# The exponents of an mLSTM: one row spread over the partitions, and columns in ScalarE's bias

## The chip, the cores and the metric

The kernel runs on one core of a Trainium2 chip. The metric is the time of one execution on the device in microseconds; the time of before is the median of three runs.

## The reference

One layer of a streaming encoder over a prompt of 2048 tokens and a batch of 8 sequences with 16 new tokens each (128 sample tokens). Model width 1024. An input projection feeds two groups of heads, the mLSTM matrix memory (4 heads of 128) and sliding-window attention (8 query heads of 64); then an output projection, LayerNorm, a convolutional feed-forward of width 2816, LayerNorm. What the change touches is the matrix memory. For one chunk, with gates `li`, `lf` per token and head and the carried state `C`, `n`, `m`:

```python
b = jnp.cumsum(lf, axis=-1)
inter = b + m[..., None]
dmat = jnp.where(causal, b[..., :, None] - b[..., None, :] + li[..., None, :], -jnp.inf)
mt = jnp.maximum(inter, jnp.max(dmat, axis=-1))
w_inter = jnp.exp(inter - mt)
s = jnp.einsum('bhld,bhsd->bhls', qc, kc) * jnp.exp(dmat - mt[..., None])
num = w_inter[..., None] * jnp.einsum('bhld,bhde->bhle', qc, C) + jnp.einsum('bhls,bhse->bhle', s, vc)
den = w_inter * jnp.einsum('bhld,bhd->bhl', qc, n) + jnp.sum(s, axis=-1)
h = num / jnp.maximum(jnp.abs(den), jnp.exp(-mt))[..., None]
```

With a = li - b and M = mt - b, three exponents are needed: a[s] - M[l] under the causal mask (128 keys by 128 queries by 4 heads), m - M[l] (the same for every partition), and -(b + M)[l]. The state goes on with the last column of the first two.

## The kernel before

The 2048 prompt tokens are 16 tiles of 128 (the kernel takes chunks of 128 tokens), the sample tokens are tile 16. `BLOCKS` groups the tiles into five input blocks, `[16, 0, 1]` first. For each block `i_block` makes the input projection: dense products of 384, 512 or 256 columns on TensorE, three passes each (`mm3`, lines 207 to 209) with operands split into a high and a low fp32r part. Then `o_block` makes the output projection per block, and the feed-forward follows (`f_ups`, `f_downs`).

The order on TensorE is written by hand. `Chains.weave` steps through the dense products and, by an estimated time, takes steps of three generators in between: `t_sample` (tile 16, first), `m_chain` (matrix memory of the prompt tiles) and `a_chain` (attention of the prompt tiles). Their `yield` gives how much of TensorE's time a step is taken for and how long its successor shall wait. VectorE, ScalarE, GpSimd and the DMA issues on SyncE are ordered by a scheduler; each engine then works through its list in order.

PSUM: the dense products rotate over three banks (`dps`); everything in the chains takes one of five banks with one tag (`bank`, tag `tb`). A tile of PSUM may be written when the bank's former content has been read.

One prompt tile of the matrix memory:

- `m_rows` transposes the gates to rows of 4 partitions x 128 (`pgr`), and VectorE scans `b`, `a`, `M` (lines 627 to 629). `hilo_rows` (564, 565) writes a in two fp32r parts into `ae` and the carried m into `me`; `hilo_rhs` (571, 572) splits M into `r_Mh` and `r_Ml`, and GpSimd multiplies each by a diagonal pattern into `re` (574, 575), which is 100 x 512. `emt_row` (579) makes the row `y` = -(b + M).
- `m_tile` loads q, k, v (`m_load`), makes the scores (`pscore`, 672) and the transposed keys (`pkt`, 683), then the exponents as one product each of 100 rows by 512 columns: `m_inter` (664, bank named `pe2`, written `pe` in the trace) for m - M, and `m_weights` (654, `pe`) for a - M. ScalarE takes the exponential of the first into `wi` (666); VectorE takes the minimum of the second and the mask into `dt` (656), ScalarE its exponential (657). `emt_cols` (585, bank `pemt`) turns `y` into columns. VectorE makes `sd` = scores x `dt` (677) and `kw` = keys x last column of `dt` (738), GpSimd `qk` = q x `wi` (736).
- After further dense work: the numerators (`pnum`, 745 and 746), the state update (`pcu`, 753, and `C`, 756), `m_norm`, and `m_out` (`pht`, 721, copied by ScalarE into `mixm`, 723).

An attention tile takes the banks `pq`, `pk` (768, 770), four `psc` for its scores, reduced on VectorE with the mask (`amx`, 815), `ppt` for transposed weights (835) and `ppo` (842, 843). Weights for the dense products are split by ScalarE (`whi`, 202) and VectorE (`wlo`, 203); `xh`, `xl` (348, 349) are the split inputs. `d_sums` (`tx`, `ty`) prepares weights of the down projection on VectorE along the way.

Of the kernel before, what the change touches and what calls it, by code (L numbers as in the profile page):

```python
# [23 lines left out]
MH = 4  # L24
# [26 lines left out]
def _consts():  # L51
    c = {}
    c["ident"] = np.eye(P, dtype=np.float32)
    l = np.arange(P)
    c["mcau"] = np.where(l[:, None] <= l[None, :], 0.0, NEG).astype(np.float32)
    c["mblk"] = np.where((l[:, None] <= l[None, :]) & (l[:, None] // DS == l[None, :] // DS), 0.0, NEG).astype(np.float32)
    ch = l[:, None] // 64
    kc = l[None, :] // 64
    own = np.where(kc <= ch, 0.0, NEG)
    prev = np.where(kc >= ch, 0.0, NEG)  # L60
    c["mswa"] = np.stack([np.concatenate([prev, own], 1), np.concatenate([own, prev], 1)], 1).astype(np.float32)
    half = 32
# [5 lines left out]
    d4 = np.zeros((MH, MH, P), np.float32)  # L68
    for h in range(MH):
        d4[h, h] = 1.0  # L70
    c["delta"] = -d4
    oz = np.zeros((100, P), np.float32)
    oz[0:4] = 1.0
    oz[96:100] = 1.0
    c["onesz"] = oz
    dz = np.zeros((100, MH, P), np.float32)
    dz[32:36] = d4
    dz[64:68] = d4
    c["deltaz"] = dz
# [110 lines left out]
class Prog:  # L190
# [295 lines left out]
    def t_setup(self):  # L486
        nc, a, tp = self.nc, self.a, self.tp

        def ld(n):
            t = self.one("k_" + n, list(a[n].shape))  # L490
            nc.sync.dma_start(t, a[n])
            return t
        nc.sync.dma_start(self.ident, a["ident"])
        self.gb = ld("gb")
        self.mcau = ld("mcau")
        self.mblk = ld("mblk")
        self.mswa = ld("mswa")
        self.delta = ld("delta")
# [4 lines left out]
        oz = self.work("hn", [100, P])  # L503
        nc.sync.dma_start(oz, a["onesz"])
        dz = self.work("kw", [100, MH, P])
        nc.sync.dma_start(dz, a["deltaz"])

        self.ae, self.me, self.re = [], [], []
        for i in range(2):
            for l, n, src, sh in ((self.ae, "ae", oz, [100, P]), (self.me, "me", oz, [100, P]), (self.re, "re", dz, [100, MH, P])):  # L510
                t = self.one(f"{n}{i}", sh, F32R)
                nc.vector.tensor_copy(t, src)
                l.append(t)
# [44 lines left out]
        self.nc.tensor.transpose(ps[:, 1], g[:, i, 4:8], self.ident)  # L558
        return ps[:, 0], ps[:, 1]

    def hilo_rows(self, dst, src):

        nc = self.nc
        nc.vector.tensor_copy(dst[32:36], src)
        nc.vector.tensor_sub(dst[64:68], src, dst[32:36].bitcast(F32))

    def hilo_rhs(self, re, M):

        nc = self.nc
        h, l = self.row("Mh", F32R), self.row("Ml")  # L570
        nc.vector.tensor_copy(h, M)
        nc.vector.tensor_sub(l, M, h.bitcast(F32))
        bc = lambda r: r.rearrange("p (o m) -> p o m", o=1).to_broadcast([MH, MH, P])
        nc.gpsimd.tensor_tensor(re[0:4], bc(h.bitcast(F32)), self.delta, op=ALU.mult)
        nc.gpsimd.tensor_tensor(re[96:100], bc(l), self.delta, op=ALU.mult)

    def emt_row(self, b, M):
        y = self.row("y")
        self.nc.vector.scalar_tensor_tensor(y, b, -1.0, M, op0=ALU.mult, op1=ALU.subtract)
        return y  # L580

    def emt_cols(self, y):

        ps = self.bank([P, MH], "pemt")
        self.nc.tensor.transpose(ps, y, self.ident[:MH, :MH])
# [37 lines left out]
    def m_rows(self, t, b, ti):  # L623
        V = self.nc.vector
        lf, li = self.gate_rows(self.logs_of(b), ti)
        bc, a_, M = self.row("b"), self.row("a"), self.row("M")
# [8 lines left out]
        self.mc = self.work("mc", [MH, 1], bufs=3)  # L635
        V.tensor_add(self.mc, bc[:, P - 1:P], M[:, P - 1:P])
        return ae, me, re, y

    def m_load(self, t, b, ti):
        nc = self.nc  # L640
# [6 lines left out]
        nc.sync.dma_start(og, self.zog[t].rearrange("p (h e) -> p h e", h=MH))  # L647
        return qk, v1, og

    def m_weights(self, ae, re, mask):  # L650

        nc = self.nc
        pe = self.bank([P, MH, P], "pe")
        nc.tensor.matmul(pe.rearrange("p h l -> p (h l)"), ae, re.rearrange("p h l -> p (h l)"), start=True, stop=True)
        dt = self.work("dt", [P, MH, P])
        nc.vector.tensor_tensor(dt, pe, mask.rearrange("p (o m) -> p o m", o=1).to_broadcast([P, MH, P]), op=ALU.min)
        nc.scalar.activation(dt, dt, AF.Exp)
        return dt

    def m_inter(self, me, re):  # L660

        nc = self.nc
        pe = self.bank([P, MH, P], "pe2")
        nc.tensor.matmul(pe.rearrange("p h l -> p (h l)"), me, re.rearrange("p h l -> p (h l)"), start=True, stop=True)
        wi = self.work("wi", [P, MH, P])
        nc.scalar.activation(wi, pe, AF.Exp)
        return wi

    def m_scores(self, qk):
# [53 lines left out]
        nc.scalar.copy(mix, ps)  # L723
        self.mix_out(t, 0, mix)

    def m_tile(self, t, b, ti, ae, me, re, y):
# [124 lines left out]
    def t_sample(self):  # L851
        nc, a = self.nc, self.a
        V = nc.vector
        t = NPT
# [6 lines left out]
        bc, a_, M, ar = [self.row(n) for n in ("b", "a", "M", "x")]  # L861
# [12 lines left out]
        self.hilo_rhs(self.re[0], x)  # L874
        self.hilo_rows(self.ae[1], a_)
        self.hilo_rhs(self.re[1], M)
        y = self.emt_row(bc, M)
# [40 lines left out]
        hn = self.m_norm(num, emt, og)  # L918
# [612 lines left out]
```

## Time and profile before

| | us |
|---|---|
| median of three runs | 2494.75 (2488.86 to 2495.19) |
| profiled execution | 2496.35 |
| its span | 2494.6 |
| TensorE busy | 2395.8 (96%) |
| VectorE busy | 1865.9 (75%) |
| ScalarE busy | 1205.2 (48%) |
| GpSimd busy | 467.2 (19%) |

The first 860 us hold the input projection, the output projection of four blocks and the three chains; the rest is the feed-forward. In the profile's rows PE is TensorE, PEld its weight loads, DVE VectorE, ACT ScalarE, POOL GpSimd, SP SyncE. A row of a timeline gives start, length, engine, line, operation and the tile written with the tiles read; in brackets stands idle time of the engine before it and what ended it. Lengths of matmuls include their latency; what one takes from the next is seen from start to start. The lines of waits give the waiting group, the releaser, the total, the count and the longest.

### The profile page before, as it was taken

The numbers are of one execution on the slowest core, as the hardware profiler recorded it, in microseconds if no ns is written. First come the engines' busy times: TensorE is split into PE (matmuls) and PEld (weight loads), VectorE is DVE, ScalarE is ACT, GpSimd is POOL, SyncE is SP. The second block draws the span as 40 slices with busy tenths as digits, with TensorE's granted clock in tenths as the row PEclk, the third lists the DMA queues.
The fourth block names the chain that finished last, engine by engine and source line by source line (L and its number), as shares of the span: only waits on it lengthen the run. The fifth ranks groups of instructions, "written<-read, shape, count | busy, mean of one in ns | idle before, by whom it ended". The sixth has DMA issues, their size and how long they took to land.

```text
span 2494.6 us, 36890 instructions
## 1 busy us (share of the span) xinstructions
PE 2395.8 (96%) x12922; PEld 2131.1 (85%) x12922; DVE 1865.9 (75%) x3244; ACT 1205.2 (48%) x2170; POOL 467.2 (19%) x486
## 2 busy tenths in 40 slices
PE   8999999999989899989999999999999999999998
PEld 8777778878887777789999999999999978778776
DVE  5656777487588887888788876678766677796897
ACT  4323445344355543555555545555544544444553
POOL 1211332132143434310000000002000010220300
PEclk9999999999998999999999999999999999999999
DMA  8886744544556567667777789886998876656653
GB/s 268 306 275 221 249 128 136 174 125 136 176 163 204 174 205 261 212 227 271 288 279 264 264 301 315 314 304 223 326 300 262 267 267 205 232 188 203 219 185 108
DMA packets 277117, 575.28 MB, mean 231 GB/s; under 512 B 45300, under 2 KB 122204, under 8 KB 276932
## 3 DMA queue, kind: packets, MB, share of 16 engines
q1 hardware_dynamic: 275204, 566.64, 67.3%
q0 software_dynamic: 1728, 6.29, 0.7%
q8 instruction: 102, 1.67, 0.3%
q14 instruction: 83, 0.68, 0.1%
HBM read 419.06 MB, written 153.78 MB: 230 GB/s over the span
## 4 chain that ended last, share of the span: by engine, by line
PE 54%; DVE 10%; issue 4%; DMA 3%; ACT 3%; POOL 2%; SPq 0%; DVEq 0%; ACTq 0%; POOLq 0%
PE dps L1240 16%; PE fup L1240 15%; PE fht L1437 5%; PE dps L1437 5%; PE fup L1437 5%; PE dps L207 2%; PE dps L209 2%; PE dps L208 2%; DVE wlo L203 2%; DMA zf<-cc 1%; ACT cc L1286 1%; DVE cc L1288 1%; DVE hl L203 1%; PE fht L1112 0%; POOL ymix L1028 0%
## 5 line engine op out<-in xcount | busy, mean ns | idle before, releaser
L1240 PE MATMUL fup<-hh,uw 128*128 128x384 f32 (+1 forms) x1848 | 483.6, 330 | 10.8 <-ACT u L1265 3.5
L1240 PE MATMUL dps<-hh,uw 128*128 128x384 f32 (+1 forms) x1848 | 481.7, 329 | 7.4 <-ACT u L1265 5.1
L203 DVE TENSOR_TENSOR wlo<-wraw,whi 128x1024 fp32r<-128x1024 f32 (+3 forms) x289 | 349.0, 1215 | 143.8 <-ACT whi L202 137.2
L202 ACT CAST whi<-wraw 128x1024 fp32r<-128x1024 f32 (+3 forms) x289 | 281.8, 981 | 310.4 <-PE dps L1437 94.0
L1240 PEld LDWEIGHTS fup<-hh,uw 128*128 128x128 f32 x1848 | 331.8, 189 | 13.9 <-ACT u L1265 4.7
L1240 PEld LDWEIGHTS dps<-hh,uw 128*128 128x128 f32 x1848 | 330.6, 188 | 9.6 <-ACT u L1265 6.6
L1288 DVE SCALAR_TENSOR_TENSOR cc<-u,cw,cc 128x768 f32<-128x768 f32 (+1 forms) x264 | 252.6, 977 | 110.6 <-ACT cc L1286 108.2
L207 PE MATMUL dps<-whi,xh 128*128 128x512 f32 (+1 forms) x816 | 317.3, 389 | 0.0
L209 PE MATMUL dps<-whi,xl 128*128 128x512 f32 (+1 forms) x816 | 310.5, 380 | 2.3 <-DVE xl L349 2.3
L208 PE MATMUL dps<-wlo,xh 128*128 128x512 f32 (+1 forms) x816 | 310.5, 380 | 2.1 <-DVE wlo L203 2.0
L1240 PE MATMUL fup<-hl,uw 128*128 128x384 f32 (+1 forms) x924 | 303.7, 329 | 1.4 <-DVE hl L203 1.4
L1240 PE MATMUL dps<-hl,uw 128*128 128x384 f32 (+1 forms) x924 | 302.7, 328 | 0.0
L1286 ACT ACTIVATE cc<-u,cw 128x768 f32<-128x768 f32 (+1 forms) x132 | 129.6, 997 | 117.7 <-DVE u L1279 58.1
L209 PEld LDWEIGHTS dps<-whi,xl 128*128 128x128 f32 x816 | 155.1, 190 | 34.1 <-DVE xl L349 2.7
L208 PEld LDWEIGHTS dps<-wlo,xh 128*128 128x128 f32 x816 | 155.7, 191 | 31.4 <-DVE wlo L203 2.9
L207 PEld LDWEIGHTS dps<-whi,xh 128*128 128x128 f32 x816 | 155.8, 191 | 30.1 <-ACT xh L348 0.4
L1240 PEld LDWEIGHTS fup<-hl,uw 128*128 128x128 f32 x924 | 174.4, 189 | 1.6 <-DVE hl L203 1.6
L1240 PEld LDWEIGHTS dps<-hl,uw 128*128 128x128 f32 x924 | 173.9, 188 | 0.0
L1437 PE MATMUL fup<-whi,fu 128*128 128x512 f32 x484 | 159.6, 402 | 6.4 <-DVE yacc L1466 4.4
L1437 PE MATMUL dps<-whi,fu 128*128 128x512 f32 x440 | 149.0, 395 | 0.0
L1280 POOL COPY u<-prev 128x4 f32<-128x4 f32 x66 | 45.3, 687 | 465.2 <-DVE cc L1288 449.9
L1437 PE MATMUL fht<-whi,fu 128*128 128x512 f32 x396 | 132.1, 396 | 0.2 <-DVE yacc L1466 0.2
(289 smaller groups left out, 4598.7 us busy)
## 6 DMA issues: line engine op xcount, KB each, us to landing
uw<-zw SPq DMA_DIRECT2D x176, 512.0 KB, 4.7
zw<-uw SPq DMA_DIRECT2D x88, 512.0 KB, 2.9
wv<-wup SPq DMA_DIRECT2D x66, 512.0 KB, 5.6
wraw<-wtm SPq DMA_DIRECT2D x60, 512.0 KB, 4.8
wraw<-zt SPq DMA_DIRECT2D x60, 512.0 KB, 4.2
wraw<-wdn SPq DMA_DIRECT2D x45, 512.0 KB, 4.0
wraw<-wqk SPq DMA_DIRECT2D x40, 512.0 KB, 5.0
wraw<-wo SPq DMA_DIRECT2D x40, 512.0 KB, 4.8
```

What stands on the lines that cost most here:

```text
L202: nc.scalar.copy(hi, src)
L203: nc.vector.tensor_sub(lo, src, hi.bitcast(F32))
L207: mm(out, ah, bh, start=start, stop=False)
L208: mm(out, ah, bl, start=False, stop=False)
L209: mm(out, al, bh, start=False, stop=stop)
L1240: mm(ps, l[:, k], r[:, k], start=s in (1, 7) and k == 0 and i == 0, stop=k == 3 and i == 2, skip_group_check=True)
L1280: nc.gpsimd.tensor_copy(u[:, :, 0:2], self.prev[:, :, j])
L1286: S.activation(c[:, v], u[:, v, 2:2 + n], AF.Identity, bias=w[3], scale=w[2])
L1288: V.scalar_tensor_tensor(c[:, v], u[:, v, i:i + n], w[i], c[:, v], op0=ALU.mult, op1=ALU.add)
L1437: mm(ps, l[:, k, c], r[:, k], start=s in (1, 4, 7) and u == 0 and k == 0 and i == 0, stop=u == nu - 1 and k == n - 1 and i == 2, skip_grou ...
```

## The change

M alone is split into two fp32r parts, in one tile `hl` of 36 partitions (high part in 0 to 3, low part in 32 to 35, zeros between, so that the sum over partitions adds both). `m_rep` spreads -M over the 128 partitions with four products of 128 columns, one for each head, from a constant `sel`; the bank `pm` serves both exponents. a and y are rows of one tile `ay` and are transposed together by TensorE into a bank `pcol`; the carried m is spread by a small product into the same bank. VectorE copies the columns to `col`, and ScalarE adds them as its per-partition bias: `wi` and `dt` become four exponentials of 128 columns each. VectorE adds the mask instead of taking the minimum. The products on GpSimd, `ae`, `me`, `re` and the constants `delta`, `onesz`, `deltaz` go; the constant `sel` and the setup of `hl` and `ay` come. On TensorE `pm` and `pcol` stand where `pe2`, `pe`, `pemt` stood, so a prompt tile takes four gate and score banks instead of five. In the sample tile `pm` is made twice, once for x = M - m.

```diff
-    def hilo_rows(self, dst, src):
+    def hilo(self, i, src):
+        nc, dst = self.nc, self.hl[i]
+        nc.vector.tensor_copy(dst[0:4], src)
+        nc.vector.tensor_sub(dst[32:36], src, dst[0:4].bitcast(F32))
+    def y_row(self, i, b, M):
+        self.nc.vector.scalar_tensor_tensor(self.ay[i][32:36], b, -1.0, M, op0=ALU.mult, op1=ALU.subtract)
+    def m_cols(self, i, mp=None):
         nc = self.nc
-        nc.vector.tensor_copy(dst[32:36], src)
-        nc.vector.tensor_sub(dst[64:68], src, dst[32:36].bitcast(F32))
-    def hilo_rhs(self, re, M):
-        nc = self.nc
-        h, l = self.row("Mh", F32R), self.row("Ml")
-        nc.vector.tensor_copy(h, M)
-        nc.vector.tensor_sub(l, M, h.bitcast(F32))
-        bc = lambda r: r.rearrange("p (o m) -> p o m", o=1).to_broadcast([MH, MH, P])
-        nc.gpsimd.tensor_tensor(re[0:4], bc(h.bitcast(F32)), self.delta, op=ALU.mult)
-        nc.gpsimd.tensor_tensor(re[96:100], bc(l), self.delta, op=ALU.mult)
-    def emt_cols(self, y):
-        ps = self.bank([P, MH], "pemt")
-        self.nc.tensor.transpose(ps, y, self.ident[:MH, :MH])
+        ps = self.bank([P, 40], "pcol")
+        if mp is not None:
+            nc.tensor.matmul(ps[:, 0:4], mp.to_broadcast([MH, P]), self.ident[:MH, :MH], start=True, stop=True)
+        nc.tensor.transpose(ps[:, 4:40], self.ay[i], self.ident[:36, :36])
+        c0 = 4 if mp is None else 0
+        col = self.work("col", [P, 8], bufs=2)
+        nc.vector.tensor_copy(col[:, c0:8], ps[:, c0:8])
         emt = self.work("emt", [P, MH], bufs=2)
-        self.nc.scalar.activation(emt, ps, AF.Exp)
-        return emt
+        nc.scalar.activation(emt, ps[:, 36:40], AF.Exp)
+        return col, emt
...
     def m_rows(self, t, b, ti):
-        ae, me, re = self.ae[t % 2], self.me[t % 2], self.re[t % 2]
-        self.hilo_rows(ae, a_)
-        self.hilo_rows(me, self.mc.to_broadcast([MH, P]))
-        self.hilo_rhs(re, M)
-        y = self.emt_row(bc, M)
+        self.hilo(i, M)
+        self.y_row(i, bc, M)
...
-    def m_weights(self, ae, re, mask):
+    def m_rep(self, i):
+        pm = self.bank([P, MH, P], "pm")
+        for h in range(MH):
+            self.nc.tensor.matmul(pm[:, h], self.sel[:, h], self.hl[i], start=True, stop=True)
+        return pm
+    def m_weights(self, pm, col, mask):
         nc = self.nc
-        pe = self.bank([P, MH, P], "pe")
-        nc.tensor.matmul(pe.rearrange("p h l -> p (h l)"), ae, re.rearrange("p h l -> p (h l)"), start=True, stop=True)
         dt = self.work("dt", [P, MH, P])
-        nc.vector.tensor_tensor(dt, pe, mask.rearrange("p (o m) -> p o m", o=1).to_broadcast([P, MH, P]), op=ALU.min)
-        nc.scalar.activation(dt, dt, AF.Exp)
+        nc.vector.tensor_tensor(dt, pm, mask.rearrange("p (o m) -> p o m", o=1).to_broadcast([P, MH, P]), op=ALU.add)
+        for h in range(MH):
+            nc.scalar.activation(dt[:, h], dt[:, h], AF.Exp, bias=col[:, 4 + h:5 + h])
         return dt
-    def m_inter(self, me, re):
-        nc = self.nc
-        pe = self.bank([P, MH, P], "pe2")
-        nc.tensor.matmul(pe.rearrange("p h l -> p (h l)"), me, re.rearrange("p h l -> p (h l)"), start=True, stop=True)
+    def m_inter(self, pm, col):
         wi = self.work("wi", [P, MH, P])
-        nc.scalar.activation(wi, pe, AF.Exp)
+        for h in range(MH):
+            self.nc.scalar.activation(wi[:, h], pm[:, h], AF.Exp, bias=col[:, h:h + 1])
         return wi
...
     def m_tile(...):
-        wi = self.m_inter(me, re)
-        dt = self.m_weights(ae, re, self.mcau)
-        emt = self.emt_cols(y)
+        pm = self.m_rep(i)
+        col, emt = self.m_cols(i, mp)
+        wi = self.m_inter(pm, col)
+        dt = self.m_weights(pm, col, self.mcau)
...
     def t_sample(self):
-        wi = self.m_inter(self.me[1], self.re[0])
-        dt = self.m_weights(self.ae[1], self.re[1], self.mblk)
-        emt = self.emt_cols(y)
+        wi = self.work("wi", [P, MH, P])
+        nc.scalar.activation(wi, self.m_rep(0), AF.Exp)
+        pm = self.m_rep(1)
+        col, emt = self.m_cols(1)
+        dt = self.m_weights(pm, col, self.mblk)
```

More of the change, by code (lines that the diff above doesn't have):

```diff
@@ L67, in _consts @@
     c["rope"] = rp.reshape(NT, P, 2, half).transpose(1, 0, 2, 3)
-    d4 = np.zeros((MH, MH, P), np.float32)
+    sel = np.zeros((36, MH, P), np.float32)
     for h in range(MH):
[L70 to L79, printed above, removed]
+        sel[h, h] = sel[32 + h, h] = -1.0
+    c["sel"] = sel
     segs = np.ones((MH, P), np.float32)
@@ L497, in t_setup @@
         self.mswa = ld("mswa")
-        self.delta = ld("delta")
         self.seg = ld("seg")
@@ L502, in t_setup @@
         self.m0 = ld("m0")
[L503 to L508, printed above, removed]
+        raw = self.work("kw", [36, MH, P])
+        nc.sync.dma_start(raw, a["sel"])
+        self.sel = self.one("sel", [36, MH, P], F32R)
+        nc.vector.tensor_copy(self.sel, raw)
+        self.hl = [self.one(f"hl{i}", [36, P], F32R) for i in range(2)]
+        self.ay = [self.one(f"ay{i}", [36, P]) for i in range(2)]
         for i in range(2):
[L510 to L513, printed above, removed]
+            nc.vector.memset(self.ay[i], 0.0)
+            nc.vector.tensor_copy(self.hl[i], self.ay[i])
         self.kh, self.kl = [self.one(n, [P, RING, P], F32R) for n in ("kringh", "kringl")]
@@ L559, in gate_rows @@
         return ps[:, 0], ps[:, 1]
-    def hilo_rows(self, dst, src):
-        nc = self.nc
-        nc.vector.tensor_copy(dst[32:36], src)
-        nc.vector.tensor_sub(dst[64:68], src, dst[32:36].bitcast(F32))
-    def hilo_rhs(self, re, M):
-        nc = self.nc
-        h, l = self.row("Mh", F32R), self.row("Ml")
-        nc.vector.tensor_copy(h, M)
-        nc.vector.tensor_sub(l, M, h.bitcast(F32))
-        bc = lambda r: r.rearrange("p (o m) -> p o m", o=1).to_broadcast([MH, MH, P])
-        nc.gpsimd.tensor_tensor(re[0:4], bc(h.bitcast(F32)), self.delta, op=ALU.mult)
[L575 to L580, printed above, removed]
-    def emt_cols(self, y):
-        ps = self.bank([P, MH], "pemt")
-        self.nc.tensor.transpose(ps, y, self.ident[:MH, :MH])
+    def hilo(self, i, src):
[5 more added lines that the diff above has]
+    def m_cols(self, i, mp=None):
+        nc = self.nc
+        ps = self.bank([P, 40], "pcol")
[5 more added lines that the diff above has]
+        nc.vector.tensor_copy(col[:, c0:8], ps[:, c0:8])
         emt = self.work("emt", [P, MH], bufs=2)
-        self.nc.scalar.activation(emt, ps, AF.Exp)
-        return emt
+        nc.scalar.activation(emt, ps[:, 36:40], AF.Exp)
+        return col, emt
     def place(self, t):
@@ L625, in m_rows @@
         lf, li = self.gate_rows(self.logs_of(b), ti)
-        bc, a_, M = self.row("b"), self.row("a"), self.row("M")
+        i = t % 2
+        bc, a_, M = self.row("b"), self.ay[i][0:4], self.row("M")
         V.tensor_tensor_scan(bc, lf, self.seg[:, 0], 0.0, op0=ALU.add, op1=ALU.add)
@@ L629, in m_rows @@
         V.tensor_tensor_scan(M, self.seg[:, 0], a_, self.mc, op0=ALU.add, op1=ALU.max)
-        ae, me, re = self.ae[t % 2], self.me[t % 2], self.re[t % 2]
-        self.hilo_rows(ae, a_)
-        self.hilo_rows(me, self.mc.to_broadcast([MH, P]))
-        self.hilo_rhs(re, M)
-        y = self.emt_row(bc, M)
-        self.mc = self.work("mc", [MH, 1], bufs=3)
+        self.hilo(i, M)
+        self.y_row(i, bc, M)
+        mp, self.mc = self.mc, self.work("mc", [MH, 1], bufs=3)
         V.tensor_add(self.mc, bc[:, P - 1:P], M[:, P - 1:P])
-        return ae, me, re, y
+        return i, mp
     def m_load(self, t, b, ti):
@@ L724, in m_out, with m_tile @@
         self.mix_out(t, 0, mix)
-    def m_tile(self, t, b, ti, ae, me, re, y):
+    def m_tile(self, t, b, ti, i, mp):
         nc = self.nc
@@ L860, in t_sample @@
         lf, li = self.gate_rows(self.logs_of(b), ti)
-        bc, a_, M, ar = [self.row(n) for n in ("b", "a", "M", "x")]
+        bc, M, ar = [self.row(n) for n in ("b", "M", "x")]
+        a_ = self.ay[1][0:4]
         V.tensor_tensor_scan(bc, self.seg[:, 1], lf, 0.0, op0=ALU.mult, op1=ALU.add)
@@ L873, in t_sample @@
         V.tensor_sub(b3(x), b3(M), self.m0.rearrange("p (b o) -> p b o", o=1).to_broadcast([MH, DB, DS]))
[L874 to L877, printed above, removed]
+        self.hilo(0, x)
+        self.hilo(1, M)
+        self.y_row(1, bc, M)
         yield 300, 10000
         qk, v1, og = self.m_load(t, b, ti)
-        wi = self.m_inter(self.me[1], self.re[0])
-        dt = self.m_weights(self.ae[1], self.re[1], self.mblk)
-        emt = self.emt_cols(y)
+        wi = self.work("wi", [P, MH, P])
[3 more added lines that the diff above has]
+        dt = self.m_weights(pm, col, self.mblk)
         sd = self.m_weighted(self.m_scores(qk), dt)
```

## The prediction

> **What bounds the kernel now.** I read the table of stages first (busy time per engine, TensorE's granted clock, DMA), then TensorE's waits in the stages that the change touches, then the timelines around the longest of those waits. The matrix memory lives in the first 860 us; its 17 tiles are woven between dense products.
>
> ```profile
> 107.00:220.00 113.00, 102.82 (x593) 83.92 (x592) 67.56 (x147) 28.75 (x68) 26.04 (x25) 0.95 0.74 250
> 220.00:400.00 180.00, 166.88 (x911) 137.95 (x910) 140.73 (x412) 81.47 (x210) 57.45 (x48) 0.97 0.58 186
> 400.00:600.00 200.00, 192.23 (x1084) 162.07 (x1084) 134.30 (x382) 93.25 (x236) 57.78 (x57) 0.99 0.46 144
> 600.00:860.00 260.00, 244.58 (x1367) 206.61 (x1366) 195.92 (x534) 128.71 (x304) 83.59 (x67) 0.95 0.55 178
> 860.00:2490.00 1630.00, 1590.43 (x8477) 1453.18 (x8475) 1269.76 (x1676) 827.17 (x1285) 229.11 (x269) 0.99 0.73 249
> ```
>
> Columns after the length: TensorE, weight loads, VectorE, ScalarE, GpSimd busy, then TensorE's clock and DMA. TensorE sets the pace in every stage; from 107 to 860 us it stands still for 753 - 706.5 = 46 us, and its clock falls to 0.95 and 0.97. After 860 us nothing changes, so a microsecond saved before it is saved at the end. What TensorE waits for before 870 us (line, releaser, total, times, longest):
>
> ```profile
> PE pkt L683 <- DVE amx L815: 6.9, 3, 2.7
> ...
> PE pemt L585 <- ACT mixm L723: 5.7, 3, 2.1
> ...
> PE psc L207 <- DVE dt L656: 2.7, 1, 2.7
> ...
> PE pe L654 <- POOL re L575: 2.5, 1, 2.5
> ...
> PE pk L770 <- DVE dt L656: 1.9, 1, 1.9
> PE pe L664 <- POOL re L575: 1.6, 1, 1.6
> ...
> PE ppo L842 <- ACT wi L666: 0.9, 3, 0.3
> ```
>
> All seven touch the gate work that the change rewrites. Two are GpSimd's products. The others are waits for one of the five shared PSUM banks, which VectorE or ScalarE has not yet read.
>
> **Part 1: the sample tile's products leave GpSimd.** TensorE's timeline (start, length, engine, line):
>
> ```profile
> 114.54 0.39 PE L208 MATMUL dps<-xl,whi 128*128 128x512 f32 x1
> 114.76 0.40 PE L209 MATMUL dps<-xh,wlo 128*128 128x512 f32 x1
> 116.74 0.51 PE L664 MATMUL pe<-re,me 100*128 100x512 f32 x1 [1.58 <-POOL re L575]
> 119.75 0.79 PE L654 MATMUL pe<-re,ae 100*128 100x512 f32 x1 [2.50 <-POOL re L575]
> ...
> 123.25 0.78 PE L207 MATMUL dps<-xh,whi 128*128 128x512 f32 x1
> ...
> 126.33 0.39 PE L208 MATMUL dps<-xl,whi 128*128 128x512 f32 x1
> ```
>
> From 114.76 to the next dense product at 123.25 pass 8.5 us. Afterwards the same stretch holds one dense product, eight `pm` products, one transpose, eight score products and four key transposes, and it waits only for VectorE's split of M; both pauses in the rows end at GpSimd. A product of 512 columns costs 0.23 us from start to start (114.54 to 114.76), one of 128 columns 0.11:
>
> ```profile
> 226.54 0.27 PE L207 MATMUL psc<-kringh,qh 64*128 64x128 f32 x1
> 226.65 0.27 PE L208 MATMUL psc<-kringl,qh 64*128 64x128 f32 x1
> ```
>
> That is 21 x 0.11 + 0.23 = 2.5 us: 6.0 us saved. The seven dense products from 123.25 to 126.33 took 3.08 us where 7 x 0.23 = 1.6 do, since the array came back at half clock: 1.4 more. Together 7.4; at least 4.7, if a VectorE step as long as `r_Ml`'s 1.27 (below) stands ahead of the split and the clock does not recover.
>
> **Part 2: VectorE is freed in front of `amx`.** The longest wait, `pkt` for a bank of the attention scores, falls three times, on the first tile of an input block. TensorE, then VectorE ahead of it:
>
> ```profile
> 319.05 0.63 PE L683 MATMUL pkt<-ident,qk 128*128 128x128 f32 x4 [2.67 <-DVE amx L815]
> ...
> 321.50 0.80 PE L207 MATMUL dps<-xh,whi 128*128 128x512 f32 x1
> ...
> 327.64 0.41 PE L209 MATMUL dps<-xh,wlo 128*128 128x512 f32 x1
> ```
>
> ```profile
> 308.70:318.10 9.40, 7.69 (x50) 6.37 (x48) 9.11 (x16) 2.45 (x4) 6.53 (x6) 1.00 0.61 202
> ```
>
> ```profile
> 312.10 1.27 DVE L572 TENSOR_TENSOR r_Ml<-r_M,r_Mh 4x128 f32<-4x128 f32 x1
> ...
> 314.80 1.19 DVE L564 CAST me<-mc 4x128 fp32r<-4x128 f32 x1
> ...
> 317.83 0.28 DVE L565 TENSOR_TENSOR me<-mc,me 4x128 fp32r<-4x128 f32 x1
> 318.13 0.42 DVE L815 CUSTOM_DVE_ANT_0 sc<-psc,k_mswa 128x256 f32<-128x256 f32 x1
> ```
>
> VectorE is busy 9.11 of the 9.4 us before the first score reduction at 318.13, so whatever leaves this stretch brings it forward. `me` goes: 1.19 + 0.28. `ae` goes: by its groups (busy, mean ns)
>
> ```profile
> L575 POOL TENSOR_TENSOR re<-r_Ml,k_delta 4x512 fp32r<-4x512 f32 x18 | 33.6, 1866 | 5.8 <-DVE r_Ml L572 5.4 <-ACT whi L202 0.3
> ...
> L565 DVE TENSOR_TENSOR ae<-r_a,ae 4x128 fp32r<-4x128 f32 x17 | 4.8, 283 | 0.5
> ...
> L564 DVE CAST ae<-r_a 4x128 fp32r<-4x128 f32 x17 | 4.1, 244 | 0.5
> ```
>
> 0.53. And `r_Ml`, a 4x128 subtraction like `ae`'s, takes 1.27 where `ae`'s takes 0.283, beside the first GpSimd product: 1.0 more. The sum is 3.0 us. The pause of 2.67 is gone. After it come `pe`, `pe`, `pemt`, paced by the following reductions: 319.05 to 321.50 is 2.45 us for 4 x 0.11 + 2 x 0.23 and 0.15 for `pemt` (368.23 to 368.38, below), 1.05 of work, so 1.4 lost. In the built program the new sequence takes four banks, not five, and its last (`pcol`) waits for the third reduction, which by then is also 3 us earlier. And from 321.50 to 327.64 14 dense products take 6.1 us instead of 3.2: 2.9 for the clock. I count 6.9 of pauses over the three places, 1.4 at each (4.2, from the first), and the clock only at the first: 14.0; I take 12, since TensorE, arriving sooner, may find part of them again. From below: if VectorE is no earlier, only the last bank's wait goes, about 0.5 each, 1.5.
>
> **Part 3: one bank fewer.** `pemt` waited 5.7 us for ScalarE's copy `mixm`. In the built program `pcol` now waits for an earlier bank and `mixm`'s bank passes to the attention transposes, which follow three dense products later (0.7 us). So 3 x 0.7 = 2 us go and the rest only moves; between 0 (ScalarE, now with more work, is later) and 5.7. The 0.9 us of `ppo` behind `wi` goes, since `wi` no longer holds a bank of its own. `psc` and `pk` behind the mask addition `dt` (4.6 us) stay waits for `dt`, but VectorE gets there 2 to 3 us earlier: I take 3.
>
> At this place the clock decides what a shortened pause is worth:
>
> ```profile
> 368.23 0.22 PE L585 MATMUL pemt<-ident,r_y 4*128 4x4 f32 x1 [2.08 <-ACT mixm L723]
> 368.38 0.62 PE L207 MATMUL dps<-xh,whi 128*128 128x512 f32 x1
> 368.80 0.63 PE L208 MATMUL dps<-xl,whi 128*128 128x512 f32 x1
> ```
>
> After a pause of 2.08 us the dense products stand 0.42 us apart, half speed. The Trainium skill ("TensorE: Matmul & The Clock Gate", Part 1, What's actually happening) has the half rate come after an idle window of about 3.4 us. By that rule this pause would have cost no clock, and any remainder below 3.4 us would be free of it. The trace disagrees, so I count no clock back where a pause of some 1.4 us is left.
>
> **Part 4: what is added.** TensorE, each of 16 prompt tiles: four `pm` products (0.44) for two of 512 columns (0.46), then the `mc` product (at most two passes of 0.11) and a transpose of 36 columns (at most 0.11) for `pemt`'s 0.15: about +0.1, bounds 0 and +0.16; 16 x 0.1 = 1.6. ScalarE: `wi` and `dt` become four exponentials of 128 columns each.
>
> ```profile
> L657 ACT ACTIVATE dt<-dt 128x512 f32<-128x512 f32 x17 | 10.7, 627 | 12.8 <-DVE dt L656 12.8
> L666 ACT ACTIVATE wi<-pe 128x512 f32<-128x512 f32 x17 | 10.0, 591 | 15.5 <-PE pe L664 15.5
> ```
>
> ```profile
> 359.90 1.28 ACT L710 ACTIVATE hn<-hn,ms 128x128 f32<-128x128 f32 x4 [6.38 <-DVE ms L708]
> ```
>
> Four such with a per-partition operand take 1.28, so a tile adds 2 x 1.28 - 1.22 = 1.3 us to ScalarE, which is half idle. But `wi` now also waits for VectorE's copy `col`, and in ScalarE's order `dt`'s exponentials and weight casts queue behind it. Who needs them: `sd` and through it `pnum`, in the second tile
>
> ```profile
> 258.88 0.69 DVE L677 TENSOR_TENSOR sd<-pscore,dt 128x512 f32<-128x512 f32 x1
> ...
> 260.55 0.39 PE L745 MATMUL pnum<-v,sd 128*128 128x129 f32 x2
> ```
>
> has 1.0 us to spare. Where TensorE comes 2 to 3 us earlier this cover is gone and VectorE's lead must replace it. For that I take 3 us, bounds 0 and 24 (1.5 in each of 16 tiles). The smaller constants and setup copies lie beside weight loads: nothing either way.
>
> **Sum.** 7.4 + 12 + 2 + 0.9 + 3 - 1.6 - 3 = 20.7 us saved. The profiled execution took 2496.35 us (span 2494.6), 1.6 above the median of the runs, 2494.75; so 2475.6 in its terms, 2474 beside the median. A measurement of this kernel can tell about 0.3% from no change, 7.5 us.
>
> **Rivals.** (a) VectorE is late before `amx` for other reasons and `r_Ml` was not slow because of GpSimd. Against: 0.283 for the same shape. Then Part 2 gives 1.5 and the `dt` term 0: 20.7 - 10.5 - 3 = 7.2 saved, 2487. (b) Every pause moves to the next wait, `pnum` or the transposes, and only the sample tile's 7.4 stays, less 1.6 and 3: 2492. For it: VectorE is 74% busy from 220 to 860 us, and the chain through it is nearly as long as TensorE's. (c) Slower: ScalarE, held in order behind `col`, makes `pnum` wait. `col` stands in VectorE's queue where the mask stood, and VectorE came to the mask so late that `psc` waited 2.7 us for it in one place. From more than 1.5 us of such waiting at most tiles (24 us), with a clock streak of 1 us behind each (16), less the 20.7 + 3 of the rest, it is 16 slower: 2511. Against it: 1 us of slack at the tightest, a half-idle ScalarE. (d) The shortened work does everything at the upper bounds: 7.4 + 14 + 5.7 + 0.9 + 4.6 - 1.6 = 31, 2463; I add a few microseconds for clock that I did not count.
>
> **Chances.** Forecast with (d) 0.68, (a) 0.10, (b) 0.09, (c) 0.13. The range reaches from (d) to (b), 2459 to 2492, leaving out (c) and some of both tails. Faster by over 0.3% is the forecast and most of (a): 0.77; within it the rest of (a) and (b): 0.11; slower 0.12.
>
> **What would show it.** Right: no TensorE wait on GpSimd `re`; less than 4 us between the dense products around the sample's gates; `pkt` waiting for `amx` under 2 us in total; the copies of `hl` near 0.2 to 0.3 us; the clock of 220 to 400 us at 0.98 or above; 600 to 860 shorter. Wrong: `pnum` waiting for `sd` or `qk` in many tiles, or weight products waiting for `whi` behind ScalarE's exponentials; `amx` still late; `pm` products above 0.11 us apart.

## The result, and the profile after

| kernel | median, us | runs | lowest to highest |
|---|---|---|---|
| before, same chip | 2495.11 | 20 | 2487.60 to 2505.37 |
| changed | 2480.72 | 20 | 2475.62 to 2494.91 |

The ratio of changed to before is 0.9947, 95% interval 0.9937 to 0.9957: 13 us, or 0.53%, faster (the two medians lie 14.4 apart). That is the forecast direction and inside the range, but two thirds of the 20.7 us that the sum gave.

The first profiled execution of the changed kernel took 2492.93 us, one of the two longest of the 20, so the profile that follows is one of a second set of runs of the same kernel (first experiment below): 2482.45 us, span 2480.7, beside a median of 2483.12.

The stages, columns as in the prediction (length; TensorE, weight loads, VectorE, ScalarE, GpSimd busy; clock; DMA):

```profile
107.00:220.00 113.00, 106.82 (x607) 87.35 (x606) 67.82 (x152) 29.75 (x73) 21.10 (x22) 0.93 0.71 249
220.00:400.00 180.00, 169.86 (x954) 141.44 (x954) 127.70 (x398) 90.11 (x257) 41.60 (x37) 0.98 0.56 185
400.00:600.00 200.00, 194.78 (x1112) 164.71 (x1111) 126.98 (x369) 99.84 (x254) 46.04 (x50) 1.00 0.48 152
600.00:860.00 260.00, 246.31 (x1409) 208.95 (x1408) 188.42 (x531) 141.20 (x350) 68.38 (x60) 0.97 0.56 185
```

From 220 to 400 us VectorE has 13 us less to do than before and GpSimd 16 less, ScalarE 9 more; TensorE is busier by 3.0, and its clock is 0.98, 1.00 and 0.97 in the last three stages, where it was 0.97, 0.99 and 0.95; in the first it is 0.93, where it was 0.95. What TensorE waits for before 870 us (total, times, longest):

```profile
PE pnum L732 <- issue: 7.9, 3, 3.3
PE pht L707 <- ACT hn L696: 7.0, 5, 2.9
...
PE pnum L732 <- DVE sd L663: 5.6, 2, 4.5
...
PE ppt L822 <- ACT emt L571: 4.2, 3, 2.0
PE ppt L822 <- ACT mixm L709: 0.9, 1, 0.9
PE pnum L893 <- DVE sd L663: 0.8, 1, 0.8
PE pk L757 <- DVE dt L643: 0.7, 2, 0.4
PE psc L199 <- ACT emt L571: 0.7, 1, 0.7
...
PE psc L199 <- DVE amx L802: 0.3, 1, 0.3
```

This list holds both halves of the answer. The waits that the prediction named (22.2 us in its seven rows) are nearly gone: no row for `re`, none for `pkt` behind `amx`, 0.7 for `pk`. All rows of that list (those of 0.2 us and more) together fell from 57.0 us in 24 rows to 42.3 in 17. But the lines of `pnum` are new: 7.9, 5.6 and 0.8, 14.3 us, where the kernel before has no row; and so are the 4.2 and 0.9 at `ppt`. The whole profile is 13.9 us shorter (span 2494.6 to 2480.7). Three of the pauses at `pnum` carry "issue", which names no releaser; in each of them `sd` had ended about 0.1 us before `pnum` began (in the third tile, below, at 327.73 and 327.83), so they too are waits for `sd`.

The sample tile, TensorE's timeline (start, length, engine, line):

```profile
115.12 0.40 PE L201 MATMUL dps<-xh,wlo 128*128 128x512 f32 x1
115.45 1.11 PE L636 MATMUL pm<-hl,sel 36*128 36x128 f32 x8
...
117.90 0.48 PE L199 MATMUL dps<-xh,whi 128*128 128x512 f32 x1
```

2.8 us between the dense products instead of 8.5. The third prompt tile, where `pkt` had stood 2.67 us, TensorE first:

```profile
318.89 0.66 PE L636 MATMUL pm<-hl,sel 36*128 36x128 f32 x4
319.48 0.38 PE L565 MATMUL pcol<-ident,mc 4*128 4x4 f32 x2
319.79 0.25 PE L566 MATMUL pcol<-ident,ay 36*128 36x36 f32 x1
319.97 0.50 PE L199 MATMUL dps<-xh,whi 128*128 128x512 f32 x1
...
327.83 0.46 PE L732 MATMUL pnum<-v,sd 128*128 128x129 f32 x2 [2.78 <-issue]
```

then ScalarE and VectorE of the same stretch:

```profile
323.31 0.49 ACT L809 ACTIVATE sc<-sc,amx 128x256 f32<-128x256 f32 x1
...
323.86 1.11 ACT L652 ACTIVATE wi<-pm,col 128x128 f32<-128x128 f32 x4
325.73 1.28 ACT L645 ACTIVATE dt<-dt,col 128x128 f32<-128x128 f32 x4 [0.76 <-DVE dt L643]
```

```profile
325.00 0.69 DVE L643 TENSOR_TENSOR dt<-pm,k_mcau 128x512 f32<-128x512 f32 x1 [0.49 <-ACT wi L652]
327.04 0.69 DVE L663 TENSOR_TENSOR sd<-pscore,dt 128x512 f32<-128x512 f32 x1 [1.34 <-ACT dt L645]
```

`pm` is on its way at 318.89, but ScalarE works through the attention's exponentials (line 809) until 323.8. Then everything runs in single file: `wi`, the mask addition `dt` on VectorE, `dt`'s exponentials, `sd`, `pnum`. The mask addition has only to read `pm`, and yet it waits for ScalarE's `wi`, which reads the same bank: in the built program the later reader of the bank waits for the earlier one. In this tile that wait is 0.49 us; before it VectorE had stood 1.69 us for the attention's exponentials, and behind it 1.34 us for `dt`'s. So the pause has moved from `pkt` to `pnum` and kept its length. The Trainium skill ("PSUM — Partial Sum Buffer", PSUM bank collisions raise a hardware error) says that the compiler's scheduler adds a dependency between two engines that touch the same 32 partitions of a bank, reads against reads included. The trace agrees. What VectorE's and ScalarE's instructions on `dt` waited for has this first line (total, times):

```profile
  ACT wi L652: 13.6, 13
```

That is 13.6 us in 13 tiles.

### The profile page after: what moved, and what is told of

It is laid out like the page before. It is cut to its first block, busy times and chain, and to the rows that moved or that the text cites. A ratio compares the mean times of both kernels' runs of the same rounds, so it can differ in the third digit from the quotient of the medians.

```text
span 2491.1 us, 37000 instructions
## 1 busy us (share of the span) xinstructions
PE 2401.5 (96%) x12992; PEld 2139.4 (86%) x12992; DVE 1824.5 (73%) x3194; ACT 1223.7 (49%) x2269; POOL 410.2 (16%) x450
## 3 DMA queue, kind: packets, MB, share of 16 engines
q8 instruction: 103, 1.69, 0.3%
## 4 chain that ended last, share of the span: by engine, by line
PE 51%; DVE 8%; DMA 4%; issue 2%; ACT 2%; POOL 1%; SPq 0%; DVEq 0%; ACTq 0%; POOLq 0%
PE fup L1229 16%; PE dps L1229 16%; PE fht L1426 5%; PE dps L1426 5%; PE fup L1426 3%; PE dps L201 2%; PE dps L199 2%; PE dps L200 2%; DVE wlo L195 1%; DMA wv<-wup 1%; DVE cc L1277 1%; DMA yacc<-zh 1%; DVE hl L195 1%; DMA zf<-cc 1%; PE fht L1101 0%
## 5 line engine op out<-in xcount | busy, mean ns | idle before, releaser
L201 PEld LDWEIGHTS dps<-whi,xl 128*128 128x128 f32 x816 | 155.3, 190 | 34.5 <-DVE xl L341 2.7
L199 PE MATMUL dps<-xh,whi 128*128 128x512 f32 (+2 forms) x320 | 122.5, 383 | 7.0 <-ACT xh L340 6.1
```

The lines of the kernel that those rows point to most:

```text
L199: mm(out, ah, bh, start=start, stop=False)
L201: mm(out, al, bh, start=False, stop=stop)
```

## The experiments

Each was timed beside the kernel before, on one chip for those sent together. Theory A: the change removes the gate pauses, and part of the gain is eaten where the chain to `sd` now ends later than the place of `pnum` in the hand-written order. The rivals were that the second profile would show something else, that ScalarE's work as such is the limit, that the bank count was the gain, and that GpSimd or VectorE alone explains it.

**The changed kernel again.**

> The changed kernel as it is, in one set of executions with the three variants below, for a second profile and a second time. Theory A (the gain is real, part of it is eaten by new waits of TensorE at pnum): 12 to 16 us under the kernel before, 2479 to 2483; in the profile, VectorE's mask addition dt idles for ScalarE's exponentials wi in most of the 16 prompt tiles (13.6 us in the first profile), and TensorE stands at pnum for some 15 us in all. Theory B (the gain is smaller than the runs said; the first profiled execution, 3.4 us shorter than that of the kernel before, was the rule): 3 to 5 us under before.

2483.12 us, ratio 0.9954 (0.9939 to 0.9970): 11 us under before, a little short of theory A's 12 to 16. The waits are those above, so B is out.

**Mask first.**

```diff
-        wi = self.m_inter(pm, col)
         dt = self.m_weights(pm, col, self.mcau)
+        wi = self.m_inter(pm, col)
```

> Only the order inside a prompt tile is changed: the mask addition and the exponentials of dt are issued ahead of the four exponentials of wi, so that wi waits for VectorE's read of the shared bank pm, not dt for ScalarE's. Theory A (the chain to sd got longer because two engines read one bank in turn, wi first): dt's wait for wi, 13.6 us in 13 tiles, goes; TensorE's pauses at pnum, 16.7 us by gaps between starts, shrink to under 8; 5 to 9 us under the changed kernel, 2472 to 2476. Theory B (sd is late because ScalarE now has eight short exponentials and is behind with the attention's, whatever their order): pauses at pnum stay over 12 us and the time stays within 3 us of the changed kernel. Theory C (the new order makes the qk product on GpSimd, which needs wi, the last to arrive): pnum pauses as long as before, with no VectorE idle time behind them.

2482.93 us, ratio 0.9961 (0.9946 to 0.9977), against 2483.12 unedited. A miss for theory A in its first form. TensorE's waits:

```profile
PE pnum L733 <- POOL qk L723: 5.9, 4, 1.8
...
PE pnum L893 <- DVE sd L663: 1.6, 1, 1.6
```

`dt` no longer waits for `wi`, and `sd` is earlier. But `pnum` needs a second operand, `qk` times `wi`, from GpSimd, and that is now the late one: theory C, though all rows at `pnum` are 11.1 us where they were 14.3. Whichever goes second on ScalarE is late, so the order between them is no cure.

**Later `pnum`.**

```diff
-        yield 1900, 4500
+        yield 1900, 6000
```

> Only the distance in the hand-written order is changed: pnum comes after 6000 instead of 4500 units of dense work, that is about 1.5 us or six dense products of 0.23 us later. Theory A (pnum stands because sd is 2 to 4.7 us later than its place in the order): pauses at pnum shrink by up to 1.5 us in each of the six tiles where they are long, 5 to 9 us under the changed kernel, less whatever the later bn_stats, hn and pht move out. Theory B (the pauses are a symptom of VectorE and ScalarE as a whole, and only move to pht or ppt): no change within 3 us, with pauses at pht or ppt grown by as much as pnum's shrink.

2469.22 us, ratio 0.9905 (0.9889 to 0.9921): 14 us under the changed kernel, more than A expected. The remaining waits at `pnum`, and `pht`:

```profile
PE pnum L732 <- DVE sd L663: 3.9, 4, 1.9
PE pht L707 <- ACT hn L696: 3.8, 2, 2.8
...
PE pnum L893 <- DVE sd L663: 2.6, 1, 2.6
```

From 14.3 to 6.5 us, and `pht` went from 7.0 to 3.8 instead of taking them over. All rows together, though, fell only from 42.3 to 37.8 us, for dense products now wait 5.6 us for `wlo`. The waits listed are a third of the 14 us; in these two profiles the largest other part is clock: ahead of the feed-forward TensorE worked at half clock for 35.1 us in the changed kernel and for 19.1 here, which is worth 8.

**GpSimd dummies.** The results of the two added products per split are used by nothing.

```diff
         nc.vector.tensor_sub(dst[32:36], src, dst[0:4].bitcast(F32))
+        bc = lambda r: r.rearrange("p (o m) -> p o m", o=1).to_broadcast([MH, MH, P])
+        nc.gpsimd.tensor_tensor(self.dead[0:4], bc(dst[0:4].bitcast(F32)), self.dl[0:4], op=ALU.mult)
+        nc.gpsimd.tensor_tensor(self.dead[32:36], bc(dst[32:36].bitcast(F32)), self.dl[32:36], op=ALU.mult)
```

> The changed kernel with two 4x512 products per gate tile put back on GpSimd, each reading the split rows of hl and writing a tile that nothing reads. Nothing waits for them except the next use of hl two tiles later and what stands behind them in GpSimd's queue. Theory A1 (part of the gain is that VectorE's small steps no longer run beside GpSimd's products: r_Ml took 1.27 us against 0.28): the VectorE steps right behind the split (the y row, the addition mc) grow from about 0.2 to over 1 us, and the kernel is 2 to 6 us slower than the changed one. Theory A2 (VectorE gains only by the steps that are gone, and GpSimd's work beside it costs nothing): within 2 us of the changed kernel and no step longer.

2503.29 us, ratio 1.0038 (1.0025 to 1.0052): 20 us slower than the changed kernel and slower than the kernel before. A1 had allowed 2 to 6. The step that grew is not the one that I named but the split's own subtraction (VectorE's groups; min/median/max in ns):

```profile
L558 DVE CAST hl<-r_M x17: 204/207/210, 111.5 to 840.7; 4x128 fp32r<-4x128 f32 x17
L559 DVE TENSOR_TENSOR hl<-r_M,hl x17: 280/1357/1382, 111.9 to 841.1; 4x128 fp32r<-4x128 f32 x17
```

and GpSimd's first product beside it:

```profile
L562 POOL TENSOR_TENSOR dead<-hl,dl x18: 1262/1374/2132, 112.0 to 841.0; 4x512 f32<-4x512 f32 x18
```

In the changed kernel the same subtraction takes a fifth of that:

```profile
L555 DVE TENSOR_TENSOR hl<-r_M,hl x17: 273/274/282, 112.7 to 822.1; 4x128 fp32r<-4x128 f32 x17
```

That is `r_Ml` of the kernel before over again. The Trainium skill ("SBUF — State Buffer", SBUF: two separate sides) describes one port pair that VectorE and GpSimd hold in turn, a VectorE instruction with two SBUF operands waiting out a whole GpSimd instruction that reads SBUF and began first. The rows agree: 1.357 us is about the 1.374 of one GpSimd product.

**The distance in the kernel before.** The same edit of the distance, `4500` to `6000`, in the kernel before.

> The kernel before with the one change of distance that made the changed kernel 14 us faster: pnum 6000 instead of 4500 units of dense work behind the gate products. Theory A (in the kernel before the pauses stand at the gate products, pkt, pe and pemt, 22 us in all, and none at pnum; the change moved part of them to pnum, and only there the distance helps): within 5 us of the kernel before, 2490 to 2500. Theory B (4500 was too short for either kernel, or the new place in the order is luckier as a whole): 8 us or more under the kernel before, below 2487.

2493.70 us, ratio 0.9997 (0.9985 to 1.0009). Nothing, as A expected: its waits stay at the gate products, and no `pnum` row appears.

```profile
PE pkt L683 <- DVE amx L815: 5.9, 4, 2.6
...
PE pe L654 <- POOL re L575: 2.5, 1, 2.5
```

So 4500 was long enough before, and it is the change that made it too short.

**VectorE dummies.** Four more subtractions, whose result nothing uses.

```diff
         nc.vector.tensor_sub(dst[32:36], src, dst[0:4].bitcast(F32))
+        for k in range(4):
+            nc.vector.tensor_sub(self.dead, src, dst[0:4].bitcast(F32))
```

> The changed kernel with four more 4x128 subtractions on VectorE behind each split of M (4 x 0.274 = 1.1 us for each of 18 splits), written to a tile that nothing reads. It gives back the time that the split's subtraction took beside GpSimd's products (1.36 against 0.274 us in the run with GpSimd dummies, which was 20 us slower than the changed kernel), without GpSimd. Theory V (the gain lies in VectorE's time in the gate stage): 10 to 20 us slower than the changed kernel, 2493 to 2503. Theory G (it lies in GpSimd's queue: the product of qk and wi, the attention's normalisation and the memset of v stood behind the gate products): less than 5 us slower, below 2488.

2490.58 us, ratio 0.9988 (0.9976 to 1.0000), between the two theories. Against 0.9947 for the changed kernel that is 0.41%, 10 us, give or take 4: 1.1 us of VectorE in the gate stage of each tile explains about half of the 20 us of the GpSimd dummies.

**Still later.** The distance `7500`.

> The changed kernel with pnum still later, 7500 units of dense work (another 1.5 us). Theory A (pnum's pauses are the distance to sd, of which 4.6 us are left in prompt tiles at 6000): pauses at pnum under 2 us in all, 0 to 5 us under the run with 6000, 2464 to 2470, unless what hangs on pnum (bn_stats, hn, pht, the next tile's gates) becomes late. Theory B (the gain at 6000 came from another accidental order of the two chains): anything from 2465 to 2490, with no relation to pnum's pauses.

2458.88 us, ratio 0.9860 (0.9844 to 0.9875): another 10 us, twice A's most. Among TensorE's waits:

```profile
PE pht L707 <- ACT hn L696: 2.7, 2, 2.1
...
PE pnum L893 <- DVE sd L663: 1.9, 1, 1.9
...
PE pnum L732 <- DVE sd L663: 0.6, 1, 0.6
```

`pnum` waits 0.6 us in the prompt tiles, as A said. But `pnum`'s rows fell only 4.0 us since 6000, so most of this second step came from other pauses that shrank with it (all rows together went from 37.8 to 28.7 us), and that was not foreseen.

**Two banks.** The `pm` products are made twice, one bank for each reader.

```diff
         pm = self.m_rep(i)
+        pm2 = self.m_rep(i)
         col, emt = self.m_cols(i, mp)
-        wi = self.m_inter(pm, col)
+        wi = self.m_inter(pm2, col)
```

> The changed kernel with the four pm products made twice into two banks, one read by ScalarE for wi and one by VectorE for dt: five banks in a prompt tile again, as in the kernel before, and neither reader waits for the other. The known price is four products of 0.14 us in 16 tiles, 9 us. Theory S (the shared bank, wi first and dt behind it, is what makes sd late): VectorE's idle time behind wi (13.6 us in 13 tiles) goes, pnum's pauses shrink by half or more, and the time stays within 5 us of the changed kernel in spite of the 9. Theory N (the bank count is what the change gained by): pauses of 4 to 8 us come back at pm, pcol or ppt, waiting for amx, mixm or emt, and the kernel is 9 to 17 us slower than the changed one, 2492 to 2500. Theory Z (neither): about 9 us slower, pauses where they were.

2480.48 us, ratio 0.9950 (0.9936 to 0.9965), within 3 us of the unedited kernel although 64 products were added.

```profile
PE ppt L823 <- DVE col L569: 3.0, 2, 1.5
PE ppt L823 <- DVE dt L643: 2.5, 1, 2.5
PE pm L636 <- DVE amx L803: 2.3, 1, 2.3
PE pnum L734 <- POOL qk L724: 1.6, 3, 0.8
PE pnum L733 <- issue: 1.5, 1, 1.5
```

Theory S holds for the waits: none of `dt` for `wi` is left, and `pnum` has some 4.5 us instead of 14.3. Waits for banks come back, as N said: 11.3 us at `pm`, `pcol` and `ppt`, where the changed kernel has 6.1. So the shared bank did cost about what a second set of products and a fifth bank cost together, and since the gain over the kernel before is still there with five banks, the count of banks was not the main gain.

**Too late.** The distance `9000`.

> The changed kernel with pnum 9000 units behind the gate products. Theory A (distance pays only as long as TensorE stands at pnum; at 7500 some 1.3 us of such pauses are left): the gain stops, 2456 to 2464, no more than 3 us from the run with 7500 on the good side. Theory B (the gains of 14 and another 10 us came from the order of the two chains as such): another 5 to 10 us, or a jump to the other side.

2463.37 us, ratio 0.9883 (0.9867 to 0.9900): the gain stops, as A said, and seems to turn back by some 4 us, though its interval overlaps that of 7500 a little (0.9844 to 0.9875). What takes over is the attention's transposes:

```profile
PE ppt L822 <- POOL sc L812: 4.9, 1, 4.9
PE ppt L822 <- DVE C L743: 2.8, 1, 2.8
```

**The sample tile alone.** In the kernel before, the sample tile's four `re` products move to VectorE.

```diff
-        self.hilo_rhs(self.re[0], x)
+        self.hilo_rhs(self.re[0], x, V)
...
-        self.hilo_rhs(self.re[1], M)
+        self.hilo_rhs(self.re[1], M, V)
```

> The kernel before with one thing changed: in the sample tile alone the four products re are made by VectorE instead of GpSimd, so that TensorE's pauses of 1.58 and 2.50 us behind GpSimd shrink to VectorE's four short products. The prediction's Part 1 by itself, without the new gate products. Theory P (a pause saved in the sample tile is saved at the end, 4.7 to 7.4 us): 2486 to 2489. Theory G (it is given back at pcs and at tile 0, as the positions of the changed kernel say, 4.75 us ahead at the sample's pht and 2.1 at tile 0's gates): 0 to 2 us.

2490.14 us, ratio 0.9988 (0.9977 to 0.9999): 3.0 us, between P and G; the interval, 0.2 to 5.7 us, reaches into both. Both pauses on GpSimd are gone (timeline, then the waits):

```profile
114.46 0.50 PE L665 MATMUL pe<-re,me 100*128 100x512 f32 x1
116.09 0.51 PE L655 MATMUL pe<-re,ae 100*128 100x512 f32 x1 [1.13 <-DVE re L576]
...
118.03 0.48 PE L207 MATMUL dps<-xh,whi 128*128 128x512 f32 x1
```

```profile
PE pcs L914 <- DVE vws L912: 9.5, 4, 6.3
```

Dense products resume at 118.03 instead of 123.25, 5.2 us earlier; `pcs` then waits 9.5 us where it waited 6.1 in the kernel before, and takes 3.4 of them back:

```profile
PE pcs L913 <- DVE vws L911: 6.1, 4, 2.8
```

**GpSimd dummies at 7500.** The edit of the GpSimd dummies and the distance of 7500 together.

> The two GpSimd products per gate tile that nothing reads, which made the changed kernel 20 us slower at the distance 4500, now at 7500. Theory A (they cost by making sd, qk and the attention's weights late, and TensorE waits for these at pnum and ppt; VectorE's own 1.1 us explain half): with pnum's cover the cost falls to 10 us or less, 2460 to 2469. Theory B (they cost by slowing VectorE's and so the dense weights' path as a whole): the cost stays near 20 us, 2476 to 2482.

2469.01 us, ratio 0.9902 (0.9886 to 0.9918): 10 us over the run with 7500, where the same products had cost 20 at 4500. A's figure, at its edge: half of their cost went through waits that distance covers. The split's subtraction is as slow as before here (median 1.357 us). What shrank can be read from the clock that each execution was granted, as a share of full speed: the span times (1 - clock), the time lost by it, averaged over the executions, is 31 us in the changed kernel and 41 with the dummies at 4500, but 25 and 24 at 7500. So about half of the 20 us was clock, and that half is gone.

**Both distances at 7500.**

```diff
-        yield 1900, 6000
+        yield 1900, 7500
```

> The changed kernel with both distances at 7500: pnum of the prompt tiles as in the fastest run so far (2459), and the sample tile's first pnum 7500 instead of 6000 units behind its gate products, where TensorE still stands 1.9 us for sd. Theory A (a pause at pnum is covered by distance in the sample tile as well): 1 to 3 us under the run with 7500 alone, 2456 to 2458, the pause at the sample's pnum gone. Theory G (what the sample tile gains is given back at pcs and tile 0, as the run with its products on VectorE showed for half of it): within 1.5 us of 2459.

2456.03 us, ratio 0.9836 (0.9816 to 0.9855), the fastest median. Its interval overlaps that of 7500 in the prompt tiles alone (0.9844 to 0.9875), and the pause at the sample's `pnum`, which A wanted gone, is still 1.6 us, so the last edit has not been shown to do anything. The version with 7500, 34.5 us under the kernel before, beats both kernels beyond doubt.

## Why the prediction was right, and where its sum was off

**Part 1, 7.4 us (at least 4.7).** The stretch behaved as said: 2.8 us between dense products, the 2.5 worked out, and no wait for GpSimd. But the term took a pause saved in the sample tile as saved at the end. Alone it is worth 3.0 us (0.2 to 5.7), which excludes the 7.4 but not the lower bound: `pcs` takes 3.4 back. In the changed kernel the lead is still 4.7 us at the sample's `pht` (171.7 against 176.4) and is gone at tile 0, where `pnum` starts later than before, at 239.61 instead of 238.91:

```profile
239.61 0.77 PE L732 MATMUL pnum<-v,sd 128*128 128x129 f32 x2 [4.51 <-DVE sd L663]
```

```profile
238.91 0.39 PE L745 MATMUL pnum<-v,sd 128*128 128x129 f32 x2
```

(the changed kernel first, then the kernel before).

**Part 2, 12 us.** `pkt` behind `amx` has gone from 6.9 us to no row, and the subtraction takes 0.274 us: right, with `r_Ml`'s cause shown by the dummies, and in the kernel before itself: its second `r_Ml` of the sample tile takes 1.38 us beside GpSimd's products and 0.28 where VectorE makes them. That undoes rival (a). It was even too small: the same GpSimd products, with nothing waiting for their results, cost 20 us, of which VectorE's 1.1 us per split makes 10, give or take 4. Counted the other way, some 10 of the 20 were lost by the clock (above), and the rest in pauses. Which pauses the share beyond VectorE's comes from is not settled. GpSimd's own queue is the candidate, since `qk` and the attention's normalisation stand behind those products; no run separates it from the shared port.

**Part 3, 5.9 us.** `ppo` behind `wi` is gone (0.9), and `psc` and `pk` behind `dt`, 4.6, have become 1.7 of `psc` and `pk` for `emt`, `amx` and `dt`: 2.9, the 3 forecast. `pemt` behind `mixm`, 5.7, became `ppt` behind `emt` and `mixm`, 5.1: 0.6, where 2 was taken. By these rows the last bank's waiter changed its name and kept its time.

**Part 4, minus 4.6 us.** Here the sum failed. TensorE: from the first key transpose to the next dense product, where no pause and no other bank comes between, pass 1.61 us (318.36 to 319.97 in the third tile), and 1.15 in the kernel before (844.03 to 845.18 in the last tile). That is 0.46 us in each of 16 tiles, 7.4 us instead of 1.6 and far above the bound of 2.6. The four `pm` products took 0.59 us in the rows of the third tile, and the `mc` product and the transpose 0.49, together 1.08 where 0.77 had been counted: the assumption that narrow products stand 0.11 us apart was wrong for those with 36 and 4 rows. What they replace took 0.79 (844.39 to 845.18) where 0.61 had been counted, and another 0.17 us passes between `pkt` and the first `pm`. ScalarE: "For that I take 3 us, bounds 0 and 24" is the term that was mis-sized; `pnum` waited 14.3. The step before it was right (the cover of 1.0 us is gone once TensorE comes 2 to 3 us earlier); what it missed is that the four `wi` exponentials and the mask addition, which had a bank each, now read one bank in turn, so that the chain behind the attention's exponentials grew while TensorE's way to `pnum` shrank. With a bank each `pnum` waits 4.5 us; how much of the rest is ScalarE's added 1.3 us per tile was not separated. So rivals (b) and (c) were half true: a pause moved to `pnum`, with ScalarE in front of it.

That the total still came out at 13 us is partly luck of opposite errors: `pnum` took 11 us more than counted, TensorE 6, and the sample tile, as measured alone, gave 4 less; with these alone nothing would have been left of 20.7. What made up for it stands in two places. Waits for VectorE that no part of the sum names (`ptl` 4.5, `asm` 4.1 and `wlo` 2.6) fell from 11.2 us to 1.2. That VectorE's relief did this is not shown: with the GpSimd dummies they are only 2.9. And the clock gave more than the 4.3 us counted. From 107 us to the first product of the feed-forward (columns as above; before, then changed):

```profile
107.00:1027.40 920.40, 868.15 (x4662) 719.56 (x4661) 670.40 (x1668) 403.50 (x921) 295.40 (x240) 0.97 0.58 189
107.00:1011.30 904.30, 866.25 (x4733) 721.51 (x4732) 629.00 (x1622) 422.06 (x1020) 237.67 (x205) 0.98 0.58 193
```

This stretch is 16.1 us shorter (the feed-forward, unchanged, took 2.2 longer in this execution). TensorE stands still 14.2 us less. By the clock in the traces it worked at half speed for 55.0 us before and for 35.1 now, worth half of the difference, 10.0. And it has 8.1 us more to do, counted at full clock: 14.2 + 10.0 - 8.1 = 16.1. One pair of profiles exaggerates the clock, which differs between executions of one kernel. Averaged over the executions on record (20 of the changed kernel, 12 of the kernel before in the next set) the span times (1 - clock) is 29.5 us against 37.6, so some 8 of the 13 us are clock.

The signs named for right are all there: `re`, the sample's gap, `pkt`, the `hl` steps of 0.2 to 0.3 us, the clock, and the stretch from 600 to 860 us: the lead on the kernel before grows in it from 6.2 us (the `pq` at 599.41 against 605.65) to 15.5 (the last `pht`, 850.08 against 865.58), so in these profiles more than half of the gain arises there. Of those for wrong, `pnum` waiting for `sd` (in six of 17 tiles) and `pm` above 0.11 us apart came true.

## What to carry to other kernels

When a pause of the pacing engine is taken away, follow the other operands of its next product back: the work that filled the pause did not get shorter, and the order written by hand was spaced for the old pause. After such a change, try the spacing again; here it was worth 24 us on top of 13, and nothing in the kernel before (at 6000, the one distance tried there). Two readers of one PSUM bank on two engines were a chain here, and small row operations on GpSimd cost 20 us even with results that nothing reads, about half of it through VectorE's two-operand subtraction beside them. Look at the granted clock as well as at the waits: some 8 of the 13 us gained here were clock.

## What the hardware showed that was not expected

A VectorE subtraction of 4x128 took 1.357 us beside a GpSimd product and 0.274 without, while the cast just before it stayed at 0.207. Half clock after a pause does not go by the pause's length alone: behind 2.78 us at 327.83 the `pnum` products followed at full rate, two in 0.30 us; behind 4.51 us at 239.61 two took 0.57; and in the kernel before a pause of 2.08 us was enough.

```profile
240.18 0.64 PE L733 MATMUL pnum<-C,qk 128*128 128x129 f32 x2
...
328.13 0.39 PE L733 MATMUL pnum<-C,qk 128*128 128x129 f32 x2
```

(Both from the changed kernel, the line behind the `pnum` products shown above.)
